# Two-layer hybrid encoder on one core: gate rows regrouped, a token-major sum of squares, constant products ahead of the first projection, and five smaller edits

## The chip, the cores and the metric

The kernel runs on one core of a Trainium2 chip. The core has a matrix engine (TensorE, PE in the rows; its weight loads are PEld), three engines for elementwise work (VectorE, DVE; ScalarE, ACT; GpSimd, POOL) and a queue of DMA transfers that SyncE (SP) issues. The metric is the time of one execution on the device in microseconds (us). Three runs of the kernel before took 1120.58, 1123.88 and 1124.38 us, so the median is 1123.88 us.

## The reference

The input x is 512 tokens by 1024 features, mem is 256 memory tokens by 1024. Two layers follow each other:

```
for l in range(DEPTH):                       # 2
    h = _rmsnorm(x, norm_g[l])
    u = h @ w_in[l]                          # 18 column groups, among them c_ig, c_fg: 8 + 8 columns
    y_a = _hgrn2_branch(...)                 # A: gated linear recurrence, both directions
    y_b = _window_attention(...)             # B: attention within +-128 tokens
    y_c = _mlstm_branch(q, k, v, o, z, ig, fg, gate_b, conv_w, norm_g)   # C: matrix memory, both directions
    y_d = _memory_attention(q, z, _rmsnorm(mem, mem_norm_g[l]), w_mem_kv[l])  # D
    x = x + concat(y_a, y_b, y_c, y_d) @ w_out[l]
return _rmsnorm(x, final_norm_g)
```

In branch C the two convolved inputs (q and k) pass a centred convolution of five taps over time. The gates are per token, direction (2) and head (4). With b the running sum of log f, a running maximum m over earlier tokens stabilises the exponentials:

```
d_inter = b + m[..., None];  m_t = jnp.maximum(jnp.max(d_intra, axis=-1), d_inter)
g = jnp.exp(d_inter - m_t)                                # weight of the state carried in
ws = jnp.exp(a - m_new[..., None]); decay = jnp.exp(b_last + m - m_new)
C = decay * C + einsum('bhs,bhsd,bhsv->bhdv', ws, kb, vb)  # state carried from chunk to chunk
```

## The kernel before

**Tiling.** x stands feature-major, 8 blocks k of 128 features by 512 tokens. Weights come in blocks of 512 KB through a ring of three buffers `wr`. Each block is split: ACT casts it to a high part `wh`, DVE subtracts that from `wr` and leaves the low part `wl`. h is split in the same way into `hi` and `lo`, and each product is three matmuls (wh with hi, wh with lo, wl with hi), so PE has 60 to 100 matmuls a block. PSUM tiles have four names, two buffers each: `pj` (projections), `tr` (transposes and spreads), `s` (scores, states), `o` (outputs).

**What sets the order.** Most work beside the projections is written as jobs, generators that yield a time. The helper class `Weave` steps a job between two matmul blocks of a projection when a given time (`G_LAT..` for the gate chain of C, `R_LAT..` for the first norm, `M_LAT..` for the memory's norm, `S_LAT..` for the states) has passed by its own count of PE time. A scheduler then orders each engine's queue by data and by priority; `high_priority` moves an instruction ahead. At the start `in_order` holds SP, ACT, DVE and POOL to program order. Each engine works through its queue strictly in order. All instructions of ACT, DVE, POOL and SP are issued by one helper, line 142, so that the trace shows them under that line; their tiles tell them apart.

**The start** (`start`, line 1401). h needs 1/rms of each token, and the first projection does not wait for it: x itself, scaled by the norm's weights, is multiplied by the first weights (tiles `o`, then `s`, then `pj`, 48 matmuls each with 512 columns), and the result is multiplied by R afterwards. R (128 x 512, the reciprocal rms of each token in all partitions) is made thus: squares of the 8 blocks on ACT and POOL, their sum over k on POOL and DVE, over partitions by four products with ones (`add_squares`, line 470), then `rms4`, `diag` and `spread` (a product of ones with a diagonal matrix, line 493), and an ACT copy out of PSUM. With R, `norm_k` (line 504) makes h: eight multiplications, of odd k on POOL and of even k on DVE, and for each an ACT scaling (`hi`) and a DVE subtraction (`lo`). The projection of the values (`pj`, line 251, 256 columns) is the first that uses h. Layer 1 makes its R and h in the same way inside the layer loop (line 1479).

**Branch C** (`group_C`, line 899). `gate_chain` (line 925) transposes the gates from tokens to rows (line 950), 4 heads of direction 0 in partitions 0 to 3 and 4 heads of direction 1 in partitions 32 to 35, each 512 long, and runs four scans over the 512 tokens (sum and maximum, two directions). Elementwise steps and exponentials follow; the results R and G go to DRAM (`rdr`, `gdr`), from where they are read back spread over partitions, the decays through `ddr` to `dec`; two tiles TA and TB are transposed back to token-major (TMA, TMB). `conv` (line 1066) applies five taps as a DVE TENSOR_SCALAR and four DVE SCALAR_TENSOR_TENSORs for each of four blocks. `states` (line 1040) transposes k, multiplies it by weights out of TMB on DVE (tile `kw`, 128 x 384, named u in the trace), and PE multiplies that by v (`s`, 129 columns).

**The end.** `out_proj` (line 1364) adds the projection to x, squares it on ACT quarter by quarter with a sum (`sq`), and multiplies by the final weights. After all, line 1542 onwards: `rms` (line 454) of each chunk c of 128 tokens, and the scaling of both halves, one on ACT, one on DVE, then two stores of 256 KB.

## Time and profile before

| | before |
|---|---|
| median of 3 runs | 1123.88 us (1120.58 to 1124.38) |
| the profiled execution | 1126.58 us |
| its span, first to last instruction | 1124.7 us, so 1.9 us lie outside it |
| PE busy | 1083.0 us, 96% of the span |
| DVE, ACT, POOL busy | 780.0 (69%), 538.7 (48%), 140.8 (13%) |
| chain of waits that ended last | PE 77%, DVE 13%, ACT 3%, issue 2%, DMA 1% |
| data read from HBM | 99.72 MB, 92 GB/s over the span |

A row of the timeline gives the start in us from the span's start, the time of the row, the engine, the line, the operation, output tile <- input tiles, the shape, how many instructions stand together, and in brackets for how long the engine had been idle before and what ended that. A time behind a group of several is that of the group. [...] "PE busy" counts a matmul at the lower clock as busy for all of its longer time.

### The profile page before, as it was taken

What the parts mean: (1) busy time and instruction counts of PE and PEld (TensorE: products, weight loads), DVE (VectorE), ACT (ScalarE), POOL (GpSimd) and SP (SyncE); (2) the same over time, 40 slices, a digit from 0 to 9 for tenths busy, and PEclk for the clock granted to TensorE, in tenths of its full rate; (3) what the DMA queues carried; (4) which work ended last, traced back from release to release, by engine and by line L of the source; (5) the groups of instructions that cost most, each with busy time, mean ns of one, the idle gap of its engine ahead of it and who ended that gap; (6) DMA issues with size and microseconds to landing.
All of it is one profiled execution on the core that took longest, in us unless ns stands there. A gap on an engine that the chain in (4) does not pass through costs nothing.

```text
span 1124.7 us, 22824 instructions
## 1 busy us (share of the span) xinstructions
PE 1083.0 (96%) x9142; PEld 972.2 (86%) x9142; DVE 780.0 (69%) x1815; ACT 538.7 (48%) x1138; POOL 140.8 (13%) x212
## 2 busy tenths in 40 slices
PE   6899999989999999999999999999899999999997
PEld 4699988989888797888788999889889788989997
DVE  7788546787476968777373676477858678687664
ACT  5544346656444444334554433376655353433443
POOL 4200000231000213011020000012200012120200
PEclk9899999999999999999999999999999999999999
DMA  7232134111221435222434221221122233362111
GB/s 260 76 114 77 57 112 133 59 58 58 94 66 56 120 105 170 92 90 87 138 129 134 76 79 56 94 78 57 40 75 78 76 90 108 94 197 86 66 38 75
DMA packets 34785, 105.44 MB, mean 94 GB/s; under 512 B 4360, under 2 KB 7816, under 8 KB 34680
## 3 DMA queue, kind: packets, MB, share of 16 engines
q1 hardware_dynamic: 33960, 101.57, 28.6%
q0 software_dynamic: 720, 2.42, 0.5%
q8 instruction: 72, 1.18, 0.4%
q14 instruction: 33, 0.27, 0.1%
HBM read 99.72 MB, written 4.26 MB: 92 GB/s over the span
## 4 chain that ended last, share of the span: by engine, by line
PE 77%; DVE 13%; ACT 3%; issue 2%; DMA 1%; POOL 0%; SPq 0%; DVEq 0%; ACTq 0%; POOLq 0%
PE pj L248 32%; PE pj L251 29%; DVE a L142 5%; PE o L248 4%; PE s L248 3%; PE s L251 3%; DVE u L142 3%; DVE wl L142 3%; PE tr L858 1%; PE o L251 1%; ACT a L142 1%; ACT wh L142 1%; ACT u L142 1%; DVE rq_t L142 1%; PE tr L1291 1%
## 5 line engine op out<-in xcount | busy, mean ns | idle before, releaser
L251 PE MATMUL pj<-wh,u 128*128 128x256 f32 x1984 | 389.2, 287 | 1.8 <-ACT u L142 1.2
L248 PE MATMUL pj<-u,wh 128*128 128x512 f32 (+1 forms) x1216 | 378.4, 392 | 1.2 <-ACT a L142 1.0
L251 PEld LDWEIGHTS pj<-wh,u 128*128 128x128 f32 x1984 | 316.7, 189 | 6.0 <-ACT u L142 1.6
L142 DVE TENSOR_TENSOR wl<-wr,wh 128x1024 fp32r<-128x1024 f32 (+1 forms) x162 | 197.0, 1217 | 132.0 <-ACT wh L142 130.9
L251 PE MATMUL pj<-wl,u 128*128 128x256 f32 x992 | 280.7, 283 | 0.0
L248 PEld LDWEIGHTS pj<-u,wh 128*128 128x128 f32 x1216 | 219.7, 191 | 43.0 <-ACT a L142 1.4
L142 ACT CAST wh<-wr 128x1024 fp32r<-128x1024 f32 (+1 forms) x162 | 164.2, 1014 | 154.4 <-PE pj L248 85.0
L248 PE MATMUL pj<-u,wl 128*128 128x512 f32 (+1 forms) x608 | 234.3, 385 | 1.8 <-DVE wl L142 1.8
L251 PEld LDWEIGHTS pj<-wl,u 128*128 128x128 f32 x992 | 188.3, 190 | 0.8 <-issue 0.3
L248 PEld LDWEIGHTS pj<-u,wl 128*128 128x128 f32 x608 | 115.4, 190 | 25.2 <-DVE wl L142 2.0
L142 DVE TENSOR_TENSOR u<-u,a 128x512 f32<-128x512 f32 (+1 forms) x104 | 74.1, 730 | 19.7 <-PE s L251 15.9
L142 POOL TENSOR_SCALAR u<-u,rB 128x256 f32<-128x256 f32 (+1 forms) x64 | 37.4, 597 | 240.6 <-DVE rB L142 137.2
L248 PE MATMUL pj<-wh,u 128*128 128x256 f32 (+1 forms) x320 | 62.8, 287 | 0.0
L248 PE MATMUL o<-u,u 128*128 128x129 f32 (+1 forms) x384 | 51.9, 281 | 2.1 <-DVE dnC L142 2.1
L248 PEld LDWEIGHTS o<-u,u 128*128 128x128 f32 x384 | 49.7, 196 | 4.7 <-issue 2.7
L142 POOL TENSOR_TENSOR u<-u,cf 128x512 f32<-128x512 f32 x16 | 24.2, 1510 | 234.1 <-DMA u<-rdr 234.1
L248 PEld LDWEIGHTS pj<-wh,u 128*128 128x128 f32 x320 | 51.0, 188 | 0.7 <-issue 0.5
L248 PE MATMUL pj<-wl,u 128*128 128x256 f32 (+1 forms) x160 | 45.3, 284 | 0.0
L142 DVE TENSOR_TENSOR u<-u,u 128x512 f32<-128x512 f32 (+2 forms) x48 | 38.8, 841 | 3.8 <-ACT a L142 2.6
L248 PE MATMUL s<-u,a 128*128 128x256 f32 (+1 forms) x224 | 41.3, 303 | 0.0
L251 PEld LDWEIGHTS s<-u,u 128*32 128x32 f32 (+1 forms) x1760 | 27.4, 115 | 14.9 <-issue 6.0
L142 DVE TENSOR_TENSOR u<-pj,u 128x256 f32<-128x256 f32 (+2 forms) x52 | 24.9, 502 | 21.4 <-PE pj L248 14.6
(212 smaller groups left out, 1440.2 us busy)
## 6 DMA issues: line engine op xcount, KB each, us to landing
wr<-in_wpk SPq DMA_DIRECT2D x154, 512.0 KB, 3.5
u<-in_xT SPq DMA_DIRECT2D x16, 256.0 KB, 4.5
u<-rdr SPq DMA_DIRECT2D x16, 256.0 KB, 4.6
u<-gdr SPq DMA_DIRECT2D x16, 192.0 KB, 4.5
u<-in_memT SPq DMA_DIRECT2D x4, 512.0 KB
xd<-u POOLq DMA_DIRECT2D x4, 512.0 KB, 5.2
u<-xd SPq DMA_DIRECT2D x4, 512.0 KB, 9.2
out<-u SPq DMA_DIRECT2D x8, 256.0 KB, 2.0
```

The source lines that it names most:

```text
L142: r = f(*args, **kw)
L248: nc.tensor.matmul(out, l, r, start=start, stop=stop)
L251: nc.tensor.matmul(out, l, r, start=start, stop=stop, skip_group_check=True)
L858: nc.tensor.transpose(pt[:, j * P:(j + 1) * P], pr[e][:, j * P:(j + 1) * P], ident)
L1291: nc.tensor.transpose(pt[:, (2 * t + i) * P:(2 * t + i + 1) * P], pr[:, i, t * P:(t + 1) * P], ident)
```

## The change

1. Twelve products of `ones` by `ones` (128 x 128, fp32) stand on PE ahead of the first projection; their result, in an `s` buffer, is not used. `ones` is set on DVE instead of POOL.
2. The first sum of squares comes from x token-major: four more loads of 512 KB on SP (behind the first four weight blocks, ahead of the two loads of mem), four ACT squarings of 128 x 1024 with an accumulated sum. The squares of the eight blocks, their additions and `add_squares` are gone.
3. The eight multiplications of h are all on DVE, in both layers. In layer 0 they are a job of their own (`norms`), joined ahead of the values' projection, and the memory norm's `spread` moves behind the gate projections.
4. The gate rows of C are (direction, chunk, head): 2 x 16 partitions, 128 long. The four scans are 16 x 128; what a chunk gets from others comes from two small PE products with constant matrices `pred`, `succ` (the constants `cf` grow from 520 to 666 columns) and a maximum over 49 columns. The exponentials of G and TB take their bias on ACT. The two tiles are transposed into one (TM), in `o` buffers. The waits by the weave's count grow from 1800, 2250, 2250, 3400 to 6500, 2500, 4500, 4500.
5. `states`: the multiplications of `kw` have high priority.
6. `conv`: the middle tap is an ACT scaling straight from PSUM instead of a DVE TENSOR_SCALAR.
7. The last norm: three quarters' squares are summed early, the rms of a chunk is worked out right behind its last quarter, the scaling is one ACT instruction of 128 x 1024 (of the last chunk 432 columns on ACT, 592 on DVE), and five stores replace eight.

```diff
-G_LAT0, G_LAT1, G_LAT2, G_LAT3, G_LAT4 = 2800, 1800, 2250, 2250, 3400
+G_LAT0, G_LAT1, G_LAT2, G_LAT3, G_LAT4 = 2800, 6500, 2500, 4500, 4500
-R_LAT0, R_LAT = 6000, 3500
-M_LAT, M_LAT2 = 20000, 2500
+R_LAT0, R_LAT = 0, 9000
+H_LAT = 1100
+M_LAT, M_LAT2 = 20000, 1500
...
-        def norm_k(x, k, R, l, h, by):
+        def norm_k(x, k, R, l, h):
             t = a2([512])
-            by.tensor_tensor(t, x, R, ALU.mult)
+            dve.tensor_tensor(t, x, R, ALU.mult)
...
+                wv.join(*jobN)                      # group_A, ahead of go(): the values
...
                                                     # gate_chain
-                dve.tensor_tensor_scan(M[0:4], L[0:4], LI[0:4], 0.0, ALU.add, ALU.max)
-                dve.tensor_tensor_scan(rev(M), rev(L), rev(LI), 0.0, ALU.add, ALU.max)
-                dve.tensor_tensor_scan(B[0:4], KM[0:4], L[0:4], 0.0, ALU.mult, ALU.add)
-                dve.tensor_tensor_scan(rev(B), rev(KM), rev(L), 0.0, ALU.mult, ALU.add)
+                dve.tensor_tensor_scan(B[0:16], one, L[0:16], 0.0, ALU.mult, ALU.add)
+                dve.tensor_tensor_scan(rev(B), ones[32:48], rev(L), 0.0, ALU.mult, ALU.add)
+                dve.tensor_tensor_scan(M[0:16], L[0:16], LI[0:16], NEG, ALU.add, ALU.max)
+                dve.tensor_tensor_scan(rev(M), rev(L), rev(LI), NEG, ALU.add, ALU.max)
+                for r, e in ends:
+                    dve.tensor_scalar(X2[r, 0:49], succ[r], B[r, e:e + 1], None, ALU.mult)
+                    dve.tensor_scalar(X2[r, 49:98], ident[r, 0:49], M[r, e:e + 1], None, ALU.mult)
                 yield 0, G_LAT3
+                mm(pS, pred, X2[0:48, 0:49], start=True, stop=False)
+                mm(pS, ones[0:48, 0:48], X2[0:48, 49:98], start=False, stop=True)
+                dve.tensor_tensor(ca[0:48], pS, gmask, ALU.add)
+                dve.tensor_reduce(mb[0:48], ca[0:48], AX.X, ALU.max)
+                dve.scalar_tensor_tensor(M[0:48], B[0:48], mb[0:48], M[0:48], ALU.add, ALU.max)
+                dve.tensor_tensor(R[0:48], B[0:48], M[0:48], ALU.subtract)
...
+                            act.activation(G[r], R[r], AF.Exp, bias=mb[r])
+                        sy.dma_start(dst[4 * d:4 * d + 4].rearrange("h (c t) -> c h t", c=NC), src[32 * d:32 * d + 16])
...
+                    act.activation(TB[r], TA[r], AF.Exp, bias=R[r, e:e + 1])
...
+                nc.tensor.transpose(pt[:, 0:112], TA[0:112], ident[0:112, 0:112])
+                nc.tensor.transpose(pt[:, 112:160], TB[0:48], ident[0:48, 0:48])
+                act.copy(tm, pt[:, 0:160])
...
+                        with tc.high_priority():    # states: kw
+                          dve.tensor_tensor(V(kw, d * 384, ...
...
+                    act.activation(accs[b], pv, AF.Copy, scale=cw[:, l, 2 * i + b, 2:3])   # conv
-                    dve.tensor_scalar(acc, xp[:, 0:512], cw[:, l, j, 0:1], None, ALU.mult)
-                    for t in range(1, 5):
+                    for t in (0, 1, 3, 4):
...
+                if n == 2:                          # out_proj, ev1
+                    dve.tensor_reduce(ss, sq[c][:, 0:3], AX.X, ALU.add)
+                    dve.tensor_scalar(ss, ss, 1.0 / D, EPS, ALU.mult, ALU.add)
+                elif n == 3:
+                    r = rms(sq[c][:, 3:4], rest[c])
+                    cut = D if c < NC - 1 else 432
+                    act.activation(xs[c][:, 0:cut], xs[c][:, 0:cut], AF.Copy, scale=r)
+                    sy.dma_start(osrc[:, c, 0:cut], xs[c][:, 0:cut])
...
+            idle = psc()[:, 0:P]                    # start
+            for _ in range(12):
+                mm(idle, ones, ones)
...
-                if k % 2 == 1:
-                    act.activation(sqs[k], x, AF.Square)
-                    if k < 6:
-                        plus(gp, k - 1, k)
-                else:
-                    gp.tensor_tensor(sqs[k], x, x, ALU.mult)
...
+            for name, ts in (("x", xt), ("mem", mt)):
+                src = a[name].rearrange("b (c p) d -> p (b c) d", p=P)
+                for c, t in enumerate(ts):
+                    sy.dma_start(t, src[:, c])
+            def squares(ts, ss):
+                for c, t in enumerate(ts):
+                    act.activation(t, t, AF.Square, accum_out=ss[:, c:c + 1])
             def rest():
+                squares(xt, sst)
                 with tc.high_priority():
-                    add_squares(sums, sqs[0], NC, True, True)
-                    dg = diag(rms4(sums[:, 0:NC]), NC)
-                yield 900, R_LAT
+                    dg = diag(rms4(sst), NC)
+                yield 0, R_LAT
...
+                jobN.append(wv.spawn("N", norms()))
...
+            def norms():
                 for k in range(8):
-                    norm_k(xs[k // 2][:, k % 2], k, R, 0, h, gp if k % 2 else dve)
+                    norm_k(xs[k // 2][:, k % 2], k, R, 0, h)
+                    yield 0, H_LAT
```

**PE around the first sum of squares.** In the following rows of before, `s_277` is the second pair of the first projections, `tr_137` the sum over partitions (four products of 128 x 1), and `tr_330` the spread that makes R.

```order
L248 MATMUL s_277<-u_5_98,wh_266 128x512
L248 MATMUL s_277<-u_9_102,wh_266 128x512
L251 MATMUL tr_137<-ones,a_31_145 128x1 x4
L248 MATMUL s_277<-u_5_98,wl_267 128x512
L248 MATMUL s_277<-u_5_98,wh_266 128x512
...
L248 MATMUL s_277<-u_10_103,wh_266 128x512
L248 MATMUL tr_330<-a_60_322,ones 128x512
L248 MATMUL s_277<-u_6_99,wl_267 128x512
L248 MATMUL s_278<-u_5_98,wh_266 128x512
```

In the changed kernel the twelve constant products are the first work, `o_150` is the first projection, `tr_328` the spread that makes R, `s_553` a small product of branch A, `tr_858` the spread of the memory's norm, and `pj_481` the values' projection, the first user of h.

```order
L258 MATMUL s_115<-ones 128x128 x12
L258 MATMUL o_150<-u_5_98,wh_130 128x512
L258 MATMUL o_150<-u_9_102,wh_130 128x512
...
L258 MATMUL s_276<-u_6_99,wh_264 128x512
L258 MATMUL tr_328<-a_57_293,ones 128x512
L258 MATMUL s_276<-u_10_103,wh_264 128x512
...
L258 MATMUL pj_387<-u_8_101,wl_382 128x512
L261 MATMUL s_553<-a_39_247,u_44_261 32x32
L258 MATMUL tr_858<-a_62_344,ones 128x256
L261 MATMUL pj_481<-wh_469,u_13_106 128x256
```

The sum over partitions is gone from PE, the constant products are new, and the memory's spread stands right ahead of the values' projection where it stood in the middle of the gates'.

**DVE behind R.** In before `a_30_140` is R, `a_42_249` and `a_43_250` take the first projections times R, the rows with a 128x512 output from `u_1` to `u_4` are multiplications of h (four; the other four are on POOL), and `u_17` to `u_20` are its low parts.

```order
L142 TENSOR_TENSOR a_42_249<-o_138,a_30_140 128x512
L142 TENSOR_TENSOR a_43_250<-o_139,a_30_140 128x512
L142 TENSOR_TENSOR a_62_335<-u_1_94,a_30_140 128x512
L142 TENSOR_TENSOR a_64_343<-u_2_95,a_30_140 128x512
...
L142 TENSOR_TENSOR a_68_359<-u_4_97,a_30_140 128x512
L142 TENSOR_TENSOR wl_411<-wr_409,wh_410 128x4x256
L142 SCALAR_TENSOR_TENSOR u_17_110<-a_62_335,pg,u_13_106 128x512
L142 SCALAR_TENSOR_TENSOR u_17_110<-a_63_339,pg,u_13_106 128x512
L142 SCALAR_TENSOR_TENSOR u_18_111<-a_64_343,pg,u_14_107 128x512
...
L142 TENSOR_TENSOR a_75_383<-s_277,a_30_140 128x512
...
L142 TENSOR_TENSOR a_85_453<-pj_415,a_30_140 128x512
```

In the changed kernel R is `a_30_152`, and `a_81_448` takes the gates' projection out of the PSUM buffer that the values' projection uses next.

```order
L152 TENSOR_TENSOR a_39_247<-o_150,a_30_152 128x512
...
L152 TENSOR_TENSOR wl_382<-wr_380,wh_381 128x4x256
L152 TENSOR_TENSOR a_63_346<-s_275,a_30_152 128x512
L152 TENSOR_TENSOR a_64_353<-u_1_94,a_30_152 128x512
L152 TENSOR_TENSOR a_65_363<-u_1_94,a_30_152 128x512
...
L152 TENSOR_TENSOR a_77_411<-u_3_96,a_30_152 128x512
L152 TENSOR_TENSOR wl_470<-wr_468,wh_469 128x4x256
L152 SCALAR_TENSOR_TENSOR u_17_110<-a_64_353,pg,u_13_106 128x512
...
L152 TENSOR_TENSOR a_80_441<-u_4_97,a_30_152 128x512
L152 TENSOR_TENSOR a_81_448<-pj_386,a_30_152 128x512
L152 TENSOR_TENSOR a_82_464<-pj_387,a_30_152 128x512
...
L152 SCALAR_TENSOR_TENSOR u_20_113<-a_80_441,pg,u_16_109 128x512
```

All eight multiplications stand on DVE, between the weights' low parts and the evacuations of PSUM, and the last low part of h (row `u_20_113<-a_80_441`) comes after `a_81_448`.

**DVE in the gate chain of layer 0.** In before `a_458` is M, `a_459` B, `a_449` R, `a_463` TA and `a_464` TB; the scans show as SCALAR_TENSOR_TENSOR of 4x512.

```order
L142 SCALAR_TENSOR_TENSOR a_458_2959<-a_448_2911,a_447_2910 4x512
...
L142 SCALAR_TENSOR_TENSOR a_458_2959<-a_448_2911,a_447_2910 4x512
L142 TENSOR_TENSOR dnB_2942<-dnB_2942,seB_2945 128x2
L142 SCALAR_TENSOR_TENSOR a_459_2960<-a_460_2963,a_448_2911 4x512
L142 RECIPROCAL rB_2949<-dnB_2942 128x2
L142 SCALAR_TENSOR_TENSOR a_459_2960<-a_460_2963,a_448_2911 4x512
L142 TENSOR_TENSOR u_437_2841<-tr_2977,u_435_2839 128x3x128
L142 TENSOR_TENSOR u_438_2842<-tr_2983,u_436_2840 128x3x128
L142 TENSOR_TENSOR a_449_2912<-a_459_2960,a_458_2959 36x512
L142 TENSOR_TENSOR a_463_3001<-a_447_2910,a_459_2960 36x512
L142 TENSOR_TENSOR a_465_3003<-a_449_2912,a_458_2959 4x384 x2
L142 TENSOR_TENSOR a_464_3002<-a_463_3001,a_449_2912 4x512 x2
```

In the changed kernel `a_456` is B, `a_455` M, `a_459` X2, `a_457` TA; `tr_3030` and `tr_3036` are attention's transposes.

```order
L152 SCALAR_TENSOR_TENSOR a_456_2973<-ones,a_454_2971 16x128
L152 TENSOR_TENSOR seB_3005<-nmB_2993,par 128x2
L152 SCALAR_TENSOR_TENSOR a_456_2973<-ones,a_454_2971 16x128
L152 SCALAR_TENSOR_TENSOR a_455_2972<-a_454_2971,a_453_2970 16x128 x2
L152 TENSOR_SCALAR a_459_2976<-cf,a_456_2973 16x49
L152 TENSOR_SCALAR a_459_2976<-cf,a_455_2972 16x49
...
L152 TENSOR_TENSOR u_470_3028<-tr_3030,u_468_3026 128x3x128
L152 TENSOR_SCALAR a_459_2976<-cf,a_455_2972 16x49
L152 TENSOR_TENSOR a_457_2974<-a_453_2970,a_456_2973 48x128
L152 TENSOR_TENSOR u_471_3029<-tr_3036,u_469_3027 128x3x128
L152 TENSOR_TENSOR a_476_3077<-o_3062,a_475_3075 64x256 x2
L152 SCALAR_TENSOR_TENSOR a_476_3077<-a_476_3077,u_198_1640 128x256
```

The scans are a quarter as long and four short TENSOR_SCALARs stand among them; attention's `u<-tr,u` (line 858 on PE reads its like) stands behind these instead of behind four scans of 4x512.

## Rows read from the trace of the kernel before

**Rows 1.** The timeline of PE from the start to the values' projection (L251).

```profile
6.61 0.79 PE L248 MATMUL o<-u,wh 128*128 128x512 f32 x1 [6.61 <-ACT u L142]
7.99 0.80 PE L248 MATMUL o<-u,wh 128*128 128x512 f32 x1 [0.59 <-DVE u L142]
...
17.62 0.50 PE L248 MATMUL o<-u,wh 128*128 128x512 f32 x1 [1.23 <-DVE u L142]
...
23.04 0.62 PE L248 MATMUL s<-u,wh 128*128 128x512 f32 x2
25.39 1.02 PE L251 MATMUL tr<-ones,a 128*128 128x1 f32 x8 [1.72 <-DVE a L142]
...
46.78 0.67 PE L248 MATMUL tr<-a,ones 128*128 128x256 f32 x2 [2.96 <-DVE a L142]
...
55.81 0.28 PE L251 MATMUL pj<-wh,u 128*128 128x256 f32 x1
```

**Rows 2.** Windows on all engines: stretch, PE, PEld, DVE, ACT, POOL busy, PEclk, DMA.

```profile
25.40:31.00 5.60, 5.60 (x20) 4.15 (x21) 2.91 (x13) 1.38 (x3) 0.00 (x0) 0.70 0.39 119
46.80:51.40 4.60, 4.60 (x13) 3.64 (x14) 1.66 (x3) 3.88 (x6) 0.00 (x0) 0.63 0.31 104
249.50:253.00 3.50, 3.50 (x19) 3.50 (x20) 3.44 (x7) 0.91 (x2) 0.38 (x2) 0.58 0.02 5
799.20:803.00 3.80, 3.78 (x22) 3.80 (x23) 3.74 (x7) 0.99 (x2) 0.67 (x2) 0.63 0.01 4
```

**Rows 3.** The timeline of DVE at the start.

```profile
6.85 0.42 DVE L142 TENSOR_TENSOR wl<-wr,wh 128x256 fp32r<-128x256 f32 x1
...
8.85 1.51 DVE L142 TENSOR_TENSOR wl<-wr,wh 128x256 fp32r<-128x256 f32 x1
...
28.63 1.22 DVE L142 TENSOR_TENSOR wl<-wr,wh 128x1024 fp32r<-128x1024 f32 x1
...
32.92 5.80 DVE L142 TENSOR_TENSOR a<-u,a 128x512 f32<-128x512 f32 x4
...
39.78 4.72 DVE L142 SCALAR_TENSOR_TENSOR u<-a,pg,u 128x512 fp32r<-128x512 f32 x7
...
53.24 0.69 DVE L142 TENSOR_TENSOR a<-pj,a 128x512 f32<-128x512 f32 x1 [1.24 <-PE pj L248]
```

**Rows 4.** The timeline of POOL, h's multiplications in layer 0.

```profile
31.76 6.42 POOL L142 TENSOR_TENSOR a<-u,a 128x512 f32<-128x512 f32 x4 [14.74 <-ACT a L142]
```

**Rows 5.** The timeline of PE at the gate chains of both layers.

```profile
240.23 0.62 PE L950 MATMUL tr<-cf,a 128*100 128x128 f32 x4 [0.78 <-DVE a L142]
...
249.46 0.88 PE L858 MATMUL tr<-cf,u 128*128 128x128 f32 x3 [2.60 <-DVE u L142]
...
789.99 0.61 PE L950 MATMUL tr<-cf,a 128*100 128x128 f32 x4 [1.18 <-DVE a L142]
...
799.22 0.66 PE L858 MATMUL tr<-cf,u 128*128 128x128 f32 x2 [2.60 <-DVE u L142]
```

**Rows 6.** The timeline of DVE at the gate chain of layer 0.

```profile
242.55 1.21 DVE L142 TENSOR_TENSOR_SCAN a<-a,a 4x512 f32<-4x512 f32 x1
...
249.70 3.70 DVE L142 TENSOR_TENSOR a<-a,a 36x512 f32<-36x512 f32 x6
```

**Rows 7.** The timeline of PE at the first states of both layers.

```profile
391.31 0.88 PE L251 MATMUL s<-u,u 128*64 128x129 f32 x12 [1.60 <-DVE u L142]
...
940.82 0.88 PE L251 MATMUL s<-u,u 128*64 128x129 f32 x12 [1.24 <-DVE u L142]
```

**Rows 8.** The timeline of PE at layer 1's first use of h.

```profile
585.99 0.39 PE L248 MATMUL pj<-u,wl 128*128 128x256 f32 x1 [1.81 <-DVE wl L142]
```

**Rows 9.** The timeline of DVE at the end.

```profile
1117.01 0.49 DVE L142 TENSOR_SCALAR u<-u,rms 128x512 f32<-128x512 f32 x1
...
1118.75 0.15 DVE L142 TENSOR_REDUCE ss<-sq 128x1 f32<-128x4 f32 x1
```

**Rows 10.** The page: one transfer from DRAM, issues and time to landing.

```profile
u<-xd SPq DMA_DIRECT2D x4, 512.0 KB, 9.2
```

More of the change, by code (lines that the diff above doesn't have):

```diff
@@ L269, in trunk @@
         invf = cf[:, 4 * P:4 * P + 8]
+        pred, succ, gmask = [cf[0:48, 4 * P + 8 + o:4 * P + 8 + o + n] for o, n in ((0, 48), (48, 49), (97, 49))]
         cu = cp.tile([P, 5 * 32 + P], U8, name="cu")
@@ L283, in trunk @@
         ones = cp.tile([P, P], F32, name="ones")
-        gp.memset(ones, 1.0)
+        dve.memset(ones, 1.0)
         Rm = cp.tile([P, 256], F32, name="Rm")
@@ L452, in proj_ch, with rms @@
                             evacs[b](pt[:, :nt])
-        def rms(parts):
-            ss = sm([1], "ss")
-            dve.tensor_reduce(ss, parts, AX.X, ALU.add)
-            r = sm([1], "rms")
-            v = sm([1], "rmsv")
-            t = sm([1], "rmst")
-            act.activation(r, ss, AF.Sqrt, bias=epst, scale=1.0 / D)
-            dve.tensor_scalar(v, ss, 1.0 / D, EPS, ALU.mult, ALU.add)
+        def rms(sq, rest):
+            r, v, t = [sm([1], x) for x in ("rms", "rmsv", "rmst")]
+            act.activation(r, sq, AF.Sqrt, bias=rest, scale=1.0 / D)
+            dve.scalar_tensor_tensor(v, sq, 1.0 / D, rest, ALU.mult, ALU.add)
             dve.reciprocal(r, r)
-            dve.scalar_tensor_tensor(t, r, v, r, ALU.mult, ALU.mult)
-            dve.tensor_scalar(t, t, -0.5, 1.5, ALU.mult, ALU.add)
-            dve.tensor_tensor(r, r, t, ALU.mult)
-            return r
-        def add_squares(ps, sq, n, first, last):
-            for c in range(n):
-                gmm(ps[:, c:c + 1], sq[:, c * P:(c + 1) * P], ones[:, 0:1], first and c == 0, last)
+            dve.tensor_tensor(v, v, r, ALU.mult)
+            dve.scalar_tensor_tensor(t, v, -0.5, r, ALU.mult, ALU.mult)
+            dve.scalar_tensor_tensor(r, t, 1.5, r, ALU.add, ALU.mult)
+            return r
         def rms4(ss, n=NC):
@@ new lines, in gate_chain @@
+                X2 = a2([98])
+                for t in (M, B, X2, TA, TB):
+                    gp.memset(t, 0.0)
+                pt = po()
+                nc.tensor.transpose(pt[0:112, 0:P], GP, ident)
+                act.copy(LI[0:48], pt[0:48, 0:P])
+                act.copy(L[0:48], pt[64:112, 0:P])
+                yield 107, G_LAT2
+                def rev(t):
+                    s = t[32:48]
+                    return bass.AP(s.tensor, s.offset + P - 1, [list(s.ap[0]), [-1, P]])
+                one = ones[0:16]
@@ L1198, in mem_norm @@
             yield 0, 0
+            spread(jobM.pop(0), Rm)
+            yield 450, M_LAT2
             mem0.append(mem_kv(0))
```

173 lines of the change are left out of this document (65 added, 108 removed).

## The prediction

> **What bounds the kernel now.** I read the page first: PE is busy for 1083.0 of 1124.7 us, and the chain of waits that ended last is PE for 77%. So time is gained only where PE stands idle or runs at the lower clock, or where a matmul goes away. Hence PE's timeline next, with every row that has a wait in brackets: 41.7 us of idle time, of which 6.6 are the time to the first matmul and 8 the end. The windows then show the granted clock behind those waits. The reader is to see three things.
>
> First, PE needs 49.2 us from the first matmul (6.61) to the values' projection (55.81), for 144 matmuls of 512 columns and a few small ones [rows 1]. From 17.62 to 23.04 there are 23 such matmuls, 0.236 us each, so 144 take 34 us. Some 15 us are lost.
>
> Second, a wait of 1.7 us and more is paid twice. After it the mean clock is 0.70 over 5.6 us, 0.63 over 4.6, 0.58 over 3.5 and 0.63 over 3.8 [rows 2]. The share below one times the stretch is the price: 1.7, 1.7, 1.5 and 1.4 us.
>
> Third, these waits end on VectorE in its own queue, not on weights from HBM [rows 1, 5, 7, 8].
>
> **Start, edits 1 to 3.** The first projection goes from 7.99 to 23.04, 15.05 us for 47 matmuls that take 47 x 0.236 = 11.1 at the full clock [rows 1]. Of the 3.95 lost, 1.23 is a wait for DVE and 2.7 the lower clock, at which the kernel begins. The twelve constant products need no input from DRAM and so run while PE waits for the first block. The wait of 6.61 is for DMA and ACT and stays. After them I take the clock as full from the first dense matmuls, about 8; at worst it rises where it did, and the 2.7 stay. The 1.23 went because DVE's subtraction of a low part takes 0.42 alone and 1.51 while POOL squares x [rows 3]; without POOL's squares and additions DVE keeps ahead. Gain 3.95, between 1.2 and 4.
>
> [...]
>
> The sum over partitions disappears: 1.72 of wait, 1.02 for its products and 1.7 of clock [rows 1, 2], in all 4.4. What could be late next is x: four loads behind the first weights. Four loads of 512 KB issued together have 9.2 us from issue to landing [rows 10]; issued from 11 to 13 (the fourth weight block has to wait for its buffer first) they land by 20 to 22. Squares, root, diagonal and spread take some 4 more, so R is there at 25 to 27, against 31.7 before (POOL starts on it at 31.76 [rows 4]). The spread's place on PE would be reached at 24; PE waits there between 0 and 2 us. I take 0.
>
> The memory's spread waited 2.96 for DVE and cost 1.7 of clock [rows 1, 2]. It stands now just ahead of the values' projection: 4.7 gone. Without anything new the values start 13.1 us earlier, at 42.8.
>
> What is late next there is DVE. Behind R it has, until PSUM is free for the values: two products of the first projection, two of the second, eight multiplications of h, one evacuation: 13 x 0.69 (the like on a free DVE); seven low parts at 4.72 / 7 = 0.67; four weights' low parts at 1.22 [rows 3]; small ones of about 0.7. Together 9.0 + 4.7 + 4.9 + 0.7 = 19.3, and from R at 25.3 that ends at 44.6; since instructions overlap by nearly 0.1, at 43.5 to 44.6. Before, the four multiplications on DVE took 5.80, or 1.45 each, beside POOL's 1.6 each, so all eight alone on DVE (5.5) take less than the four did [rows 3, 4]. The values start at about 44.2, and the start gains 11.6. Its ends are 5 (clock as before, R at 27, another wait with its clock) and 13.
>
> **Gate chain, edit 4.** In layer 0 PE waits 0.78 for the rows' transpose and 2.60 for attention's `u`, and then loses 1.5 of clock; in layer 1 it waits 1.18 and 2.60 and loses 1.4 [rows 2, 5]: 4.9 and 5.2. DVE is held by four scans of 1.21 and six elementwise operations of 0.62, 8.5 us in one stretch [rows 6]. A short operation costs 0.15 [rows 9], so a scan over 128 instead of 512 columns costs 0.15 + 1.06 / 4 = 0.42; four make 1.7. The other nine lie between 0.15 and 0.62; at 0.3 they make 2.7. Together 4.4 instead of 8.5, and attention's operations find only 0.42 in front of them at a time. The longer waits given to the chain place its transposes some microseconds later, behind what they wait for, so I take the 10.1 as gone; at worst new waits give it all back (a rival below). ACT's four short exponentials instead of two long ones are hidden by PE.
>
> [...]
>
> **States and taps, edits 5 and 6.** The first states wait for DVE's weighting of k, 1.60 and 1.24 [rows 7]. With priority the weighting stands ahead of a tap and not behind; one tap fewer per block shortens the queue besides. The middle tap goes to ACT, idle for half the span. Gain 2.8, between 0 and 2.8, no clock counted.
>
> **Layer 1's start, edit 3.** PE waits 1.81 for a low part of weights [rows 8] behind multiplications of h that run beside POOL. Alone on DVE eight take 5.5 where before DVE and POOL were held for more than 6 (in layer 0 6.42 [rows 4]). The wait and its clock (as behind the like ones, 1.4 to 1.7 [rows 2]) make 3.5. As DVE now has four more multiplications to do, the lower end is a loss of 1.
>
> **End, edit 7.** The last addition stands behind a scaling of 0.49 that moves to ACT, and a reduction of 0.15 leaves the last chain [rows 9]; with a shorter scaling I take 0.8, between 0 and 1.3. Five stores instead of eight keep SP off the end.
>
> **Sum.** 11.6 + 4.9 + 5.2 + 2.8 + 3.5 + 0.8 = 28.8. Against the profiled execution, 1126.6 (span 1124.7 and 1.9 around it), that is 1097.8. The runs' median is 2.7 lower than that execution, which gives 1095.1; I add 0.9 for the clock behind the values' wait for DVE, which may or may not fall (1.7 if it does). Forecast 1096.
>
> **Rivals.**
> (a) The start gives half. DVE becomes the bound from R on: with R at 27 and operations at full length the values start at 46.3, PE has waited 3.5, the clock falls (1.7), and if it also rises late in the first projection (2.7) the start gains 13.1 - 7.9 = 5.2. Time 1102. For: DVE is full from R on. Against: the pitch is shorter than the rows' lengths. Chance 0.2. That the constant products do nothing belongs here; alone it costs 2.7.
> (b) The gate chain waits in another place. Its new step, DVE to PE and back for the maxima over chunks, and the transpose of TB behind ACT put PE in two waits of 1.5 to 2.6 per layer, each with 1.5 of clock: up to 10.1 back, time 1106. For: two more crossings between engines. Against: each stands behind 2 to 4 us more of projection than the chain needs. Chance 0.12.
> (c) Slower: SP is blocked. The stores of R and G stand in SP's queue and wait for DVE and ACT; what is behind them, weights, starts later. The ring holds three blocks, 60 to 100 matmuls each, so 15 us of PE work or more; the chain has to hold SP for that and 15 us longer in each layer to eat the 28.8, as the gates wait longer by the weave's count. Against: each block's load stood with time to spare, and PE shows no wait for a weight's DMA. From 15 us beyond the ring per layer it decides; at 18 the time is 1131. Chance 0.03.
> (d) A large gain at the start and no more: states and layer 1's start keep their waits (6.3 back): 1102. Chance 0.1.
> The forecast itself has 0.55, with 1090 to 1100 as its own range.
>
> **How the numbers follow.** The range takes in (a), (d) and most of (b) above, and below the start's and the end's upper ends with a median of 1095.1 and no clock lost: 1087 to 1109. What a measurement of this kernel can tell from no change is about 0.5%, 5.6 us: faster means below 1118.3. That takes the loss of over 20 of the 28.8, so (b) together with (a): 0.04 for no change. Slower needs (c): 0.03. Faster 0.93.
>
> **What would show it.** Right: twelve products on PE ahead of the first projection, no pitch above 0.3 us from about 8 on, no row `tr<-ones,a`, the values' first row at 43 to 45, a wait there under 2 us; no wait of 2.6 in either gate chain and clock 0.9 or more in the windows there; DVE's scans at 0.3 to 0.5; no wait over 0.5 for the first states nor at layer 1's first use of h; POOL without h. Wrong: values at 50 or later; a wait of PE for `wr` or for the spread of R; waits of PE at the small products of 49 columns; SP's loads bunched behind the stores of the gate rows.

## The result, and the profile after

The changed kernel takes 1097.64 us in the median of 4 runs (1095.96 to 1098.01) against 1124.13 us of the kernel before in the same comparison: ratio 0.9764, 95% interval 0.9735 to 0.9792. The forecast was 1096 in 1087 to 1109. The profiled execution has a span of 1094.2 us. PE is busy for 1070.1 us of it, where it was 1083.0 of 1124.7; its idle time fell from 41.7 to 24.1 us.

Where the time came from is read at places that both programs have. E5 and e9 below are second profiles of the two kernels; they stand beside the first, because the first profile of before turned out to hold much low clock: its mean clock of 0.987 is the lowest level that any of 27 further runs of that kernel shows. PE is busy for 1083.0 us in the first profile of before and for 1077.0 in the second, while its idle time is 41.7 and 43.1. Starts of rows, in us:

| place | before, first / second profile | after, first / second | gain, first pair / second pair |
|---|---|---|---|
| first row of the values' projection | 55.81 / 54.79 | 44.73 / 44.96 | 11.1 / 9.8 |
| attention's transposes released by POOL, layer 0 | 194.78 / 193.80 | 183.16 / 183.49 | 0.5 / 0.5 |
| spread of layer 1's R | 575.19 / 573.40 | 556.31 / 556.27 | 7.3 / 6.9 |
| the same transposes, layer 1 | 743.87 / 742.17 | 721.99 / 721.96 | 3.0 / 3.1 |
| PE's last matmul | 1116.39 / 1111.77 | 1086.38 / 1086.56 | 8.1 / 5.0 |
| end of the span | 1124.7 / 1120.1 | 1094.2 / 1094.3 | 0.5 / 0.6 |

The last column is the gain between a place and the one above it. The third line holds layer 0's gate chain and states, the fifth layer 1's. The sums are 30.5 and 25.8 us.

PE's timeline of the changed kernel, columns as in [rows 1]: start, length, operation, and in brackets the idle time before and what ended it.

```profile
1.06 4.32 PE L258 MATMUL s<-ones 128*128 128x128 f32 x24 [1.06 <-DVE ones L152]
6.49 0.49 PE L258 MATMUL o<-u,wh 128*128 128x512 f32 x1 [1.12 <-ACT u L152]
8.41 0.51 PE L258 MATMUL o<-u,wh 128*128 128x512 f32 x1 [1.42 <-DVE u L152]
...
19.41 0.63 PE L258 MATMUL s<-u,wh 128*128 128x512 f32 x2
```

The products fill 1.1 to 5.4. Two waits follow, 1.12 and 1.42. From 8.41 the matmuls run on without a gap, and the second projection starts at 19.41 where it started at 23.04 [rows 1]; 47 matmuls in 11.0 us are the 0.234 that before kept up without a wait only from 17.62 on. Further on, the same view:

```profile
24.09 1.12 PE L258 MATMUL tr<-a,ones 128*128 128x512 f32 x2
...
44.73 0.36 PE L261 MATMUL pj<-wh,u 128*128 128x256 f32 x1 [0.82 <-DVE a L152]
...
246.85 0.26 PE L1011 MATMUL o<-cf,a 48*128 48x48 f32 x1 [0.71 <-ACT a L152]
...
373.10 1.54 PE L261 MATMUL s<-u,u 128*64 128x129 f32 x24
...
380.19 1.54 PE L261 MATMUL s<-u,u 128*64 128x129 f32 x24 [0.65 <-DVE u L152]
...
568.80 0.51 PE L258 MATMUL pj<-u,wh 128*128 128x256 f32 x2 [1.33 <-ACT u L152]
...
785.88 0.26 PE L1011 MATMUL o<-cf,a 48*128 48x48 f32 x1 [0.84 <-ACT a L152]
...
919.61 1.54 PE L261 MATMUL s<-u,u 128*64 128x129 f32 x24 [0.65 <-DVE u L152]
```

The row `tr<-ones,a` with its wait of 1.72 [rows 1] is gone, and the spread of R (24.09) waits 0.22. The values wait 0.82 for `a` on DVE. The waits of 2.60 in the gate chains [rows 5] are gone; 0.71 and 0.84 for the second tile's transpose (L1011), which waits for ACT, are new. Each layer has two groups of states. The first (373.10, and the like at 912.54 in layer 1) has no wait where it had 1.60 and 1.24 [rows 7]; the second (380.19 and 919.61) has a new one of 0.65, where the kernel before had none. At layer 1's first use of h PE waits 1.33 for ACT where it waited 1.81 for DVE [rows 8]. Windows of the changed kernel (PE, PEld, DVE, ACT, POOL busy, PEclk, DMA), behind the waits that are left:

```profile
8.40:12.00 3.60, 3.59 (x15) 2.92 (x16) 3.60 (x8) 3.58 (x9) 0.00 (x0) 1.00 1.07 398
...
246.80:251.00 4.20, 4.15 (x34) 4.10 (x35) 2.85 (x7) 2.98 (x8) 0.94 (x2) 1.00 0.02 6
```

PEclk, the granted clock as a share of full speed, is 1.00 in both, against 0.58 to 0.70 behind the waits in [rows 2]; no other stretch before the end reads lower. One caution for the start: in the first profile of before the window from 8.40 to 12.00 reads 1.00 although the matmuls stand 0.43 us apart there (9.86, 10.29), where from 18.19 on they stand 0.23 apart. So at the start the pitch (the time from one matmul's start to the next) has to be read. DVE at the start:

```profile
26.49 1.29 DVE L152 TENSOR_TENSOR a<-o,a 128x512 f32<-128x512 f32 x2 [0.31 <-ACT a L152]
...
37.63 1.29 DVE L152 TENSOR_TENSOR a<-u,a 128x512 f32<-128x512 f32 x2
...
43.89 1.29 DVE L152 TENSOR_TENSOR a<-pj,a 128x512 f32<-128x512 f32 x2
```

It goes on without a gap of idle time from R (26.49) to the evacuation of the gates' PSUM (43.89), which releases the values. (In e5 the values wait 0.44, and what ends last there is ACT's copy of the memory's spread, `Rm`; DVE's evacuation ends shortly before it.) Two multiplications of h take 1.29, where four took 5.80 beside POOL [rows 3]. And in the gate chain:

```profile
235.23 0.41 DVE L152 TENSOR_TENSOR_SCAN a<-ones,a 16x128 f32<-16x128 f32 x1
235.66 0.86 DVE L152 TENSOR_TENSOR_SCAN a<-a,a 16x128 f32<-16x128 f32 x2
```

A scan takes 0.41 to 0.43 where it took 1.21 [rows 6].

### The profile page after: what moved, and what is told of

Its sections match the earlier page's. It is cut to its first block, busy times and chain, and to the rows that moved or that the text cites. A ratio compares the mean times of both kernels' runs of the same rounds, so it can differ in the third digit from the quotient of the medians.

```text
span 1094.2 us, 22817 instructions
## 1 busy us (share of the span) xinstructions
PE 1070.1 (98%) x9148; PEld 962.3 (88%) x9148; DVE 752.9 (69%) x1819; ACT 545.3 (50%) x1152; POOL 108.9 (10%) x184
## 4 chain that ended last, share of the span: by engine, by line
PE 78%; DVE 12%; ACT 4%; DMA 3%; issue 1%; POOL 0%; SPq 0%; ACTq 0%; DVEq 0%; POOLq 0%
PE pj L258 34%; PE pj L261 27%; DVE u L152 4%; PE s L258 4%; PE o L258 4%; DVE a L152 3%; PE s L261 3%; DVE wl L152 2%; PE o L261 2%; ACT u L152 1%; PE tr L862 1%; ACT a L152 1%; ACT wh L152 1%; DMA u<-in_memT 1%; DMA u<-in_xT 1%
## 5 line engine op out<-in xcount | busy, mean ns | idle before, releaser
L152 DVE TENSOR_TENSOR wl<-wr,wh 128x1024 fp32r<-128x1024 f32 (+1 forms) x162 | 194.4, 1201 | 123.1 <-ACT wh L152 122.0
L258 PEld LDWEIGHTS pj<-u,wh 128*128 128x128 f32 x1216 | 216.8, 188 | 44.1 <-ACT u L152 2.1
L152 ACT ACTIVATE u<-u,nmB 128x256 f32<-128x256 f32 (+1 forms) x64 | 35.8, 561 | 8.7 <-DVE nmB L152 6.5
L152 ACT COPY u<-u 128x512 f32<-128x512 f32 x40 | 26.8, 686 | 26.4 <-DVE u L152 13.0
```

What stands on the lines that cost most here:

```text
L152: r = f(*args, **kw)
L258: nc.tensor.matmul(out, l, r, start=start, stop=stop)
```

## The experiments

All but e9 and e10 start from the changed kernel. "Low clock" means stretches in which PEclk reads below 1.

**E1, without the products.** Edit:

```diff
-            idle = psc()[:, 0:P]
-            for _ in range(12):
-                mm(idle, ones, ones)
```

> The changed kernel without its twelve constant products. Theory (they raise PE's clock before the first projection): the first projection's matmuls stand about 0.43 us apart up to 13 us instead of 0.23, 2.7 us are lost there, the wait of 0.82 for DVE ahead of the values' projection is swallowed, values at 46.6 instead of 44.73, time 1099.5. Rival (they do nothing, the pitch of the first projection was set by POOL beside DVE): pitch 0.25 or less from 8.4 us on, values at 44.7, time 1097.6.

Measured: 1099.57 (1097.22 to 1100.60, 4 runs), some 2 us more than the changed kernel (1097.64, e5 1097.16). The times alone do not settle it: the intervals of the ratios to before overlap (0.9764 to 0.9818, and 0.9735 to 0.9792), so the rows decide. PE's timeline at the start of e1, and DVE's where it waits for mem:

```profile
8.37 0.79 PE L258 MATMUL o<-u,wh 128*128 128x512 f32 x1 [0.66 <-DVE u L152]
...
9.38 1.05 PE L258 MATMUL o<-u,wh 128*128 128x512 f32 x2
...
12.43 0.39 PE L258 MATMUL o<-u,wl 128*128 128x512 f32 x1
...
45.63 0.36 PE L261 MATMUL pj<-wh,u 128*128 128x256 f32 x1 [0.43 <-ACT Rm L152]
...
83.67 0.66 PE L261 MATMUL s<-u,u 128*32 128x32 f32 x32 [2.04 <-DVE rr L152]
```

```profile
76.97 0.48 DVE L152 SCALAR_TENSOR_TENSOR u<-u,pg,Rm 128x256 f32<-128x256 f32 x1 [2.00 <-DMA u<-in_memT]
```

The pitch is 0.43 up to 11.5 and 0.23 from 12.4, so the first projection ends 1.6 us later without the products (the second starts at 21.00 for 19.41). The values start only 0.9 later, as the wait of 0.82 for DVE is swallowed. Most of the rest of this profile's 4.6 us comes at 83.67, where PE waits 2.04 for DVE, as DVE had waited 2.00 for the load of mem's transpose; behind it the clock falls (0.61 from 83.6 to 88.0 us). That profile is the slowest of the four runs. DVE waits for the same load in programs with the products too, 0.43 in the changed kernel, 2.10 in e2 and 2.34 in e3, so it isn't likely to be the products' doing; it comes back in e11.

**E2, the sum of squares of before.** The squares are back on ACT and POOL, with `add_squares`, and the four loads of x token-major are gone:

```diff
+                if k % 2 == 1:
+                    act.activation(sqs[k], x, AF.Square)
...
+                else:
+                    gp.tensor_tensor(sqs[k], x, x, ALU.mult)
...
-                squares(xt, sst)
+                    add_squares(sums, sqs[0], NC, True, True)
```

> The changed kernel with the sum of squares of before (squares on ACT and POOL, additions, sum over partitions on PE); the products and the rest stay. Theory (R's time decides, because DVE is full behind R): PE waits 1 to 2 us for the sums and pays 1.0 for them and 1.7 of clock, R comes at 30 or later instead of 26.5, DVE's part behind it ends 4 to 5 us later, values at 49 to 50, time 1102 to 1103. Rival (only PE's own loss counts): values at 47.5, time 1100.3.

Measured: 1103.86 (1102.90 to 1104.73, 4 runs). PE's timeline:

```profile
16.96 0.50 PE L258 MATMUL o<-u,wh 128*128 128x512 f32 x1 [1.22 <-DVE u L152]
...
23.06 0.62 PE L258 MATMUL s<-u,wh 128*128 128x512 f32 x2
25.48 1.05 PE L261 MATMUL tr<-ones,a 128*128 128x1 f32 x8 [1.79 <-DVE a L152]
...
50.72 0.28 PE L261 MATMUL pj<-wh,u 128*128 128x256 f32 x1
```

The values start at 50.72, 6.0 later than in the changed kernel, and the time is the theory's, but its reason is not: no wait stands ahead of the values, so PE's own losses made it. They are larger than the rival's because the first projection ends at 23.06 instead of 19.41 although the clock is up from 8: DVE beside POOL puts in two waits of 1.22. That is 3.65 of the 6.0. The sums, with their wait of 1.79 and a fall of the clock behind it (0.51 from 26.7 to 30.2 us), take the other 2.3, net of the two waits of the changed kernel (0.22 and 0.82) that e2 has not. R did come late, at 31.8 us, as the theory said, but DVE was not full behind it: it stood idle for 1.62, 0.73 and 0.89 us there.

**E3, h's odd multiplications on POOL.**

```diff
-            dve.tensor_tensor(t, x, R, ALU.mult)
+            (gp if k % 2 else dve).tensor_tensor(t, x, R, ALU.mult)
```

> The changed kernel with h's multiplications of odd k on POOL again in both layers. Theory (beside POOL a multiplication takes DVE 1.45 us, so half of them beside POOL take longer than all of them alone): values 1 us later, at 45.7; in layer 1 PE's wait at the first use of h grows from 1.33 to about 2 with a fall of the clock, 2.4 us more; time 1100 to 1101. Rival (DVE is the bound and POOL relieves it): values at 43.9, layer 1 without a wait, time 1096.

Measured: 1101.20 (1098.95 to 1102.02, 4 runs). PE's timeline, two windows, and DVE's timeline of e3:

```profile
8.13 0.80 PE L258 MATMUL o<-u,wh 128*128 128x512 f32 x1 [0.47 <-DVE u L152]
...
44.15 0.35 PE L261 MATMUL pj<-wh,u 128*128 128x256 f32 x1
...
567.25 0.39 PE L258 MATMUL pj<-u,wl 128*128 128x256 f32 x1 [1.81 <-DVE wl L152]
```

```profile
8.00:12.00 4.00, 3.87 (x10) 3.11 (x11) 3.55 (x9) 4.00 (x9) 0.00 (x0) 0.58 1.05 378
567.20:571.00 3.80, 3.75 (x19) 3.75 (x20) 3.80 (x5) 0.37 (x1) 0.00 (x0) 0.57 0.61 192
```

```profile
36.59 1.88 DVE L152 TENSOR_TENSOR a<-u,a 128x512 f32<-128x512 f32 x3
...
558.47 5.21 DVE L152 TENSOR_TENSOR a<-u,a 128x512 f32<-128x512 f32 x3
```

In layer 0 the rival was right: with POOL the values start at 44.15 without a wait, although the first projection ran 1.2 us later. In layer 1 the theory was right, the wait of 1.81 for `wl` and the low clock come back, and up to layer 1's attention e3 loses 3.0 us against the changed kernel (a transpose at 765.48 for 762.29, where they stood 0.1 apart at 511). The fall is that of one execution, but all four times lie above the eight of the changed kernel. So edit 3 pays in layer 1 only.

DVE's rows say why. In layer 0 POOL's four multiplications run from 27.13 to 33.25, and DVE does other work meanwhile; its own four come later, from 35.39 on, and three of them take 1.88. In layer 1 three stand beside POOL's and take 5.21. What made h slow was that DVE's multiplications met POOL's, not that POOL had some.

**E4, the gate chain of before.** The functions' old text with rows of 512, `TMA` and `TMB`, and

```diff
-G_LAT0, G_LAT1, G_LAT2, G_LAT3, G_LAT4 = 2800, 6500, 2500, 4500, 4500
+G_LAT0, G_LAT1, G_LAT2, G_LAT3, G_LAT4 = 2800, 1800, 2250, 2250, 3400
```

> The changed kernel with the gate chain of before (4 rows of 512, its waits by the weave's count); the rest stays. Theory (scans of 1.21 and operations of 0.62 hold attention's operations on DVE): waits of 2.6 before attention's transposes return in both layers, and 0.8 to 1.2 before the rows' transpose, with 1.5 of clock each; 8 to 9 us more, time 1106. Rival (the waits came from where the chain stood beside the memory and h jobs, which has moved): under 3 us more, time 1100.

Measured: 1105.15 (1104.33 to 1106.16, 4 runs), 7.5 to 8 us more. PE's timeline:

```profile
228.79 0.61 PE L954 MATMUL tr<-cf,a 128*100 128x128 f32 x4 [0.79 <-DVE a L152]
...
238.03 0.52 PE L862 MATMUL tr<-cf,u 128*128 128x128 f32 x3 [2.61 <-DVE u L152]
...
772.73 0.61 PE L954 MATMUL tr<-cf,a 128*100 128x128 f32 x4 [0.94 <-DVE a L152]
...
781.97 0.87 PE L862 MATMUL tr<-cf,u 128*128 128x128 f32 x3 [2.60 <-DVE u L152]
```

The four waits of before return, to 0.24 us each [rows 5], in a program whose start is the new one. They belong to the chain.

**E5, the changed kernel again.**

> The changed kernel itself once more, on the chip of e6 to e8. Theory (a wait lets the clock fall in some executions and not in others): the same waits as in its first profile within 0.5 us each, but some stretch of 3 to 4 us at the lower clock behind one of them, where the first profile had none; time 1096 to 1099, longer where the mean clock is lower. Rival (the fall belongs to the place): no stretch at the lower clock again, times within 0.5 us.

Measured: 1097.16 (1096.11 to 1097.73, 4 runs). The second profile shows the waits of the first (1.33 and 0.83 to 0.01, the spread of R 0.77 instead of 0.22, branch C's 432.00 1.54 for 1.05) and again no stretch of low clock before the end. For these two profiles the rival stands, but the four runs' mean clocks are 0.998, 0.997, 0.997 and 0.996 in the order of their times. Other experiments speak for the theory, at places that their edits don't touch. In branch C's part the clock fell in e2 at a wait of 1.24 (0.51 from 439.7 to 443.2 us), in e7 at one of 0.67 (0.53 from 433.6 to 437.2), and in e6 at one of 1.25 (0.51 from 970.8 to 974.3); the mean clocks of these three profiles are 0.995, 0.996 and 0.995, against 0.998 in both of the changed kernel. The changed kernel has waits of 0.81 to 1.54 around the same instructions, and no fall in either profile.

**E6, the middle tap on DVE; e7, no priority for the states' weighting.**

```diff
-                    act.activation(accs[b], pv, AF.Copy, scale=cw[:, l, 2 * i + b, 2:3])
+                    dve.tensor_scalar(acc, xp[:, 0:512], cw[:, l, j, 0:1], None, ALU.mult)
...
-                        with tc.high_priority():
```

> The changed kernel with the convolution's middle tap on DVE again (one more TENSOR_SCALAR of 0.48 and a longer chain for each of four blocks, per layer). Theory (the states wait because of DVE's queue): PE's wait at the first states grows from 0.65 to 1.1 or more in both layers, time 1 us longer than e5. Rival (priority of the states' weighting alone does it): waits at 0.65, the same time as e5.

> The changed kernel without the priority of the states' weighting. Theory (a tap of 0.7 us stands ahead of it again): waits at the first states of 1.2 to 1.6 in both layers, 1.5 us longer than e5. Rival (the tap on ACT alone does it): waits at 0.65, the same time as e5.

Measured: e6 1096.40 (1095.17 to 1098.65), e7 1098.83 (1098.51 to 1098.96), 4 runs each, beside e5's 1097.16. PE's states, of e6 and then of e7:

```profile
373.75 1.54 PE L261 MATMUL s<-u,u 128*64 128x129 f32 x24
...
380.36 1.54 PE L261 MATMUL s<-u,u 128*64 128x129 f32 x24 [0.16 <-DVE u L152]
```

```profile
374.80 0.88 PE L261 MATMUL s<-u,u 128*64 128x129 f32 x12 [1.10 <-DVE u L152]
...
916.06 0.88 PE L261 MATMUL s<-u,u 128*64 128x129 f32 x12 [1.07 <-DVE u L152]
```

Both expectations took the 0.65 for the wait of the first states; it belongs to the second. Without the priority the first states wait 1.10 and 1.07 again and the second 0.31 and 0.30, and the time is 1.7 us longer: the states' gain is edit 5. With the tap on DVE the first states have no wait either, so the priority does that alone, and the wait of 0.65 at the second is not longer but gone (0.16 in layer 0, none in layer 1). Both expectations of e6 were wrong on the waits: the tap on ACT buys nothing that the runs can tell, and with it PE waits some tenths more. DVE's order fits that: in the changed kernel a weight's subtraction of 1.22 us (378.36) stands right ahead of the second weighting of k (379.49); in e6 the longer row of taps has pushed it behind (weighting 379.67, subtraction 380.60). No run changed that order alone.

**E8, the last norm of before.** `rms` over four quarters at the end, halves on ACT and DVE, eight stores.

```diff
-                    act.activation(xs[c][:, 0:cut], xs[c][:, 0:cut], AF.Copy, scale=r)
+            r = rms(sq[c])
```

> The changed kernel with the last norm of before (sum of four quarters at the end, scaling in halves, eight stores). Theory: from PE's last matmul to the end 0.5 to 0.8 us more than in the changed kernel, where it is 7.8; nothing else changes. Rival (the end hangs on the stores' landing alone): the same within 0.2 us.

Measured: 1097.34 (1096.95 to 1098.13, 4 runs), no difference to e5 that the runs can tell. In the profiles the last matmul starts 8.1 us before the end (1087.18 of 1095.3), against 7.8 and 7.7 in the two of the changed kernel and 8.3 in the two of before: the edit is worth 0.3 to 0.6.

**E9, the kernel before again; e10, the kernel before with the twelve products.**

> The kernel before once more, one look. Theory (the waits belong to the program, the falls of the clock behind them to chance): the eight long waits of its first profile within 0.5 us each, but fewer or other stretches at the lower clock than the seven behind waits in the first profile, and a time between 1119 and 1124. Rival (each wait of 1.7 us and more brings its fall): the same seven stretches, 1126.

> The kernel before with the twelve constant products alone. Theory (with the sums of squares on POOL, DVE's pace bounds the first projection, and the products pay only together with edit 2): pitch 0.23 behind 8 us, but new waits for DVE of over 1 us; the second projection (tiles s) starts at 23.0 as before; time as the kernel before within 0.5 us. Rival (the two edits add up): it starts at 20.4, time 2.7 us less.

E9: 1121.99, span 1120.1. Its waits and the windows behind them:

```profile
248.46 0.52 PE L858 MATMUL tr<-cf,u 128*128 128x128 f32 x3 [2.61 <-DVE u L142]
...
389.22 0.88 PE L251 MATMUL s<-u,u 128*64 128x129 f32 x12 [1.68 <-DVE u L142]
...
797.52 0.52 PE L858 MATMUL tr<-cf,u 128*128 128x128 f32 x3 [2.60 <-DVE u L142]
```

```profile
248.50:252.00 3.50, 3.50 (x31) 3.50 (x32) 3.44 (x7) 0.91 (x2) 0.38 (x2) 1.00 0.02 5
389.20:393.00 3.80, 3.78 (x30) 3.04 (x31) 3.80 (x8) 0.54 (x2) 1.39 (x3) 0.64 0.00 0
...
797.50:801.30 3.80, 3.78 (x33) 3.80 (x34) 3.74 (x7) 1.00 (x2) 0.68 (x2) 1.00 0.01 4
```

The wait of 2.61 at 248.46 is the one of [rows 5], but the clock behind it reads 1.00 here and read 0.58 there [rows 2]; the same holds at 797.52. Behind 389.22 the clock falls here, and it did not in the first profile. The waits of over 1 us repeat within 0.4 us, and of the falls behind waits there are three instead of seven. The theory holds: a wait belongs to the program, a fall behind it comes in one execution and not in the next. It isn't the chip either: in e10, in the same comparison as e9, the clock fell behind the same wait (2.55 at 250.95; 0.53 from 250.9 to 254.5 us). The runs beside the experiments say the same: within one comparison, on one chip, before ranged from 1119.5 us at a mean clock of 0.996 to 1126.4 at 0.987.

E10: 1125.44 (1120.66 to 1129.30, 10 runs) against 1123.39 (13 runs), ratio 1.0013, interval 0.9990 to 1.0036: no difference. PE's timeline and a window of the profiled execution:

```profile
17.65 0.50 PE L248 MATMUL o<-u,wh 128*128 128x512 f32 x1 [1.22 <-DVE u L142]
...
23.06 0.62 PE L248 MATMUL s<-u,wh 128*128 128x512 f32 x2
```

```profile
8.00:12.00 4.00, 3.97 (x11) 3.11 (x12) 4.00 (x5) 4.00 (x10) 3.20 (x3) 0.59 1.07 385
```

The second projection starts at 23.06, as before. The products alone gain nothing. This profile does not show the theory's reason, though: the pitch was to be 0.23 behind 8 us, and here the clock was back at the low level from 8.7 to 12.1, with waits for DVE of 0.73 and 1.22. E2, where the clock stayed up, and e9 show it better. In e9 the pitch drops to 0.23 at 11.4 us, in the first profile of before at about 13.5; yet e9's second projection starts at 23.34, no earlier, as PE waits for DVE 0.95 at 15.04 and 1.22 at 17.92.

**E11, five more edits.** Each aims at one wait that is left. The first block's products at the start come in the order wh with hi, wl with hi, wh with lo; mem's squares stand in `norms()` behind R's copy; the load of mem's transpose is issued ahead of three weight blocks, where the memory's job is spawned; the last wait of the gate chain grows; the middle tap is on DVE as in e6.

```diff
+                    for pt, c in cs:
+                        mm(pt, wl[:, c], hi, start=False, stop=False)
+                    for pt, c in cs:
+                        mm(pt, wh[:, c], lo, start=False, stop=False)
...
+                    if k == 2:
+                        squares(mt, ssm)
...
+                    memt.append(mem_load())
...
-G_LAT0, G_LAT1, G_LAT2, G_LAT3, G_LAT4 = 2800, 6500, 2500, 4500, 4500
+G_LAT0, G_LAT1, G_LAT2, G_LAT3, G_LAT4 = 2800, 6500, 2500, 4500, 6500
```

> The changed kernel with five more edits: the first block's products in an order that leaves its low part of x for last, mem's squares on ACT behind R's copy, mem's transposed load ahead of three weight blocks, G_LAT4 6500 instead of 4500, the middle tap on DVE again. Theory (each wait left in the changed kernel costs its length): 0.7 from the first, 0.5 to 0.8 ahead of the values' projection, 0.5 at the small products of branch A near 81 us, 1.4 at the transpose of TB in both layers, 1.3 at the first states: 4 us less than e5, 1093. Rival (a wait removed turns up at the next point where DVE or ACT is late): under 1 us less, 1096.5.

Measured: 1094.41 (1093.40 to 1094.62, 4 runs), ratio to before 0.9739, interval 0.9713 to 0.9766; span 1091.6. It is faster than the kernel before, and probably faster than the changed kernel: its slowest run lies 1.3 us below the fastest of the changed kernel (1095.96, e5 1096.11), but those ran in other comparisons, and the intervals of the ratios to before overlap (by 0.003 with the first, 0.002 with e5's). How much it is ahead is known only roughly, about 2.8 us by the medians. E6, which shares the tap, has a run of 1095.17 too. PE's timeline of e11:

```profile
7.74 0.74 PE L258 MATMUL o<-u,wl 128*128 128x512 f32 x2 [0.32 <-DVE wl L152]
...
24.84 1.12 PE L258 MATMUL tr<-a,ones 128*128 128x512 f32 x2 [1.24 <-DVE a L152]
...
44.28 0.47 PE L261 MATMUL pj<-wh,u 128*128 128x256 f32 x1
...
254.30 0.41 PE L863 MATMUL tr<-cf,u 128*128 128x128 f32 x2 [0.64 <-DVE u L152]
...
379.19 1.54 PE L261 MATMUL s<-u,u 128*64 128x129 f32 x24 [0.33 <-DVE u L152]
...
792.42 0.41 PE L863 MATMUL tr<-cf,u 128*128 128x128 f32 x2 [0.71 <-DVE u L152]
```

Between theory and rival. The wait of 1.42 at the start is down to 0.32, but the spread of R now comes sooner than R's diagonal and waits 1.24, so the values start only 0.45 earlier. The waits at TB's transposes are gone, and attention's transposes behind them wait 0.64 and 0.71 for DVE. The wait near 81 us is gone without a successor: mem's load had been late.

## Why the prediction was right, point by point

**The start.** Forecast 11.6 us, values at 44.2; measured 11.1 and 9.8, values at 44.73. The steps held in kind. R came at 26.5, at the late end of 25 to 27, since ACT squares mem ahead of R's copy, which I had not counted. DVE's list, reckoned at 19.3 us and less for overlap, took 18.1 (26.49 to 43.89 and one evacuation), and PE waited 0.82 for its end.

What I had wrong is whose the 2.7 us of the first projection were. I gave them to the products and only the 1.23 to POOL's leaving. E2 and e9 show that with POOL squaring an earlier clock brings nothing, as DVE's pace then fills in waits, and e10's times agree. E1 takes the two edits apart: without the products the second projection starts at 21.00, so edit 2 alone brings it 2.0 us forward from 23.04, and the products bring it 1.6 further, of which 0.9 arrive at the values. So edit 2 pays alone, and the products pay only with it. That the start came out so near the forecast is partly luck, as two of its terms stood at the wrong edit. That the products secure the clock is not so either: in four of the ten profiles with them, e3, e6, e8 and e10, it was back at the low level somewhere from 8 to 12 us (0.58 in e3's window), behind the same two waits between the products and the dense work that the changed kernel's first profile has without a fall.

**The gate chain.** Forecast 10.1 for both layers. The waits went as told, the scans took 0.41 to 0.43 for an estimated 0.42, and new waits of 0.71 and 0.84 took a little back. That is rival (b), with one wait a layer for its two, 1.55 us in all against up to 10.1, and without a fall of the clock. The small products of 49 columns wait for nothing. With the states the two layers gained 15.4 and 11.9 by the two pairs of profiles, for 12.9 forecast; e4 alone 7.5 to 8.

**The states.** Forecast 2.8 for edits 5 and 6 together; the first states' waits of 1.60 and 1.24 went, two of 0.65 at the second states came, so 1.54 net, and e7 puts 1.7 us on the priority. Edit 6, which I took for part of it, is worth nothing that the runs can tell (e6).

**Layer 1's start.** Forecast 3.5, measured 3.0 and 3.1. The wait for DVE went and one of 1.33 for ACT came: PE needs a PSUM buffer that ACT copies out at 568.38, and that copy stands behind the cast of a weight block (567.43, 1.04 us). The clock's fall was saved in both pairs. By waits and clock I can account for 2.4 of the 3; the rest is open.

**The end.** Forecast 0.8, measured 0.5 and 0.6.

**The sum.** Its terms came to 28.8; the two pairs of profiles give 30.5 and 25.8, the medians 26.5. The difference between the pairs is the clock: seven falls against three in the profiles of before, and 6.0 us of PE's busy time. I took each fall of the clock behind a wait as a fixed price, 8.0 us in all without the first projection. The profile of before on which I worked was one of its slowest executions (mean clock 0.987); over three comparisons 27 runs of before lie between 1119.5 us at 0.996 and 1127.0 at 0.987. A usual execution has fewer falls to lose, so the 28.8 read from that profile is 2.3 more than the medians gave. That is why the forecast came out low, by 1.6 us. The 0.9 that I had added for a fall behind the values' wait offset part of it, though that fall did not come; that was luck.

**The signs.** Those named for being right held, but for two: at layer 1's first use of h PE waits 1.33 where 0.5 was allowed, and although the pitch stayed at 0.23 from 8.4 us on in the first profile, the clock was up there in only six of the ten profiles with the products. Of those named for being wrong, PE waits for the spread of R, by 0.22 and 0.77.

**The rivals.** (a) came true in part: DVE is the bound behind R, with 0.8 us. (d) did not: the first states' waits went, and layer 1's start gained 3.0. (c) did not: no wait of PE for weights. But the memory's transposed load went behind two more weight blocks on SP, from 64.4 us to 69.2, and DVE waited 0.4 to 2.3 us for it in the changed kernel and its variants, which reached PE near 81 us. That is the same kind of mechanism, small, and in a place where I did not look.

## What to carry to other kernels

Read the clock behind a wait in at least two profiles before it is entered into a sum as a price: the wait repeats, the fall behind it need not (in the two profiles of before the waits of over 1 us repeat within 0.4 us, and the falls are seven and three). Where two things bound a stretch (here the clock and DVE's pace beside GpSimd), removing one may show nothing, as the products alone did (ratio 1.0013 in e10); test edits together before one is dropped. An engine that carries the wait was relieved here by what stands directly ahead of the awaited instruction (priority, 1.7 us in e7; shorter scans, with the rest of edit 4 7.5 to 8 in e4), and not by moving work from it at large (the tap, nothing that e6 can tell).
